# Attention on one core: V loaded in 8 KB runs, reordered by ScalarE and turned by VectorE instead of shuffled by matmuls

## The chip, the cores and the metric

The kernel runs on one core of a Trainium2 chip. Times are device microseconds (us) of a whole execution. An execution can fall in a slower state (for a program on one core: over 1.5% above the fastest run of the same kernel). A profile covers one execution and gives its **span**, which is 1.7 to 3.1 us shorter than the time of the same run. Engines: PE is TensorE, PEld its weight loads, DVE VectorE, ACT ScalarE, POOL GpSimd, SP SyncE; a q after a name is the queue of the engine that issues transfers.

## The reference

```
q, k, v: (32, 12, 128, 64) float32, normal * 0.1
scores = q @ k^T / sqrt(64)
attn   = exp(scores - max);  attn /= sum(attn) + 1e-8
out    = attn @ v            # float32
```

There are 384 heads of 128 rows by 64. Both kernels leave out the maximum (the scores are small) and work in bf16. They read 37.75 MB and write 12.58 MB, 50.3 MB in all. A **step** is 32 heads; there are twelve, 0 to 11, and each loads 1.05 MB each of Q, K and V and stores 1.05 MB.

## The kernel before

Q, K and V are loaded by GpSimd's queue, which casts f32 to bf16 on the way; only the first V comes uncast by two other queues. A Q or K row of 8 KB (a quarter of a head, 32 rows) goes to one partition. V comes in runs of 2 KB (8 rows), and 448 matmuls with a 0/1 matrix `perm` put it in order; ScalarE casts their results back from PSUM (on-chip accumulator memory).

```
def load_v(m):                                   # 2 KB runs, 512 of them
    ...
    nc.gpsimd.dma_start(
        out=chunks[m // 2, 2][:, m % 2 * CB:(m % 2 + 1) * CB],
        in_=vr[:, m * CB:(m + 1) * CB, :].rearrange("p n (t d) -> p n t d", t=T))
...
def turn(m, which):                              # VectorE: 32x32 blocks of 4-byte words
    ...
    nc.vector.transpose(
        xt.rearrange("p h (x g) -> p x h g", g=4),
        x if which == 0 else x.rearrange("p (y t) e -> p t y e", t=T))
...
def values(m, a, heads, half):                   # V's shuffle
    ...
                nc.tensor.matmul(
                    v_ps[u * 32:(u + 1) * 32, i], lhsT=perm[:, a + i, tl, :],
                    rhs=v_bf[:, ns, 2 * u + tl, :], start=(tl == 0), stop=(tl == 1), ...)
    nc.scalar.copy(v2s[m][:, a:a + heads, ns], v_ps)
```

The main loop is software-pipelined: step m+1's scores and exponentials (`scores`, two halves) stand beside step m's denominators and outputs. Each half has one matmul group, then one exponential of 128x2048. The order in the program is the order on each engine. Stores of finished steps are held back by about five steps (LAG), and loads are issued five steps ahead (AHEAD):

```
held = {m: [m - LAG] for m in range(LAG, e - 3)}             # e = 11
between = {(e - 3, 0): [e - 8], (e - 3, 1): [e - 7], (e - 2, 0): [e - 6],
           (e - 2, 1): [e - 5, e - 4], (e - 1, 0): [e - 3]}
...
for m in range(NDUO):
    if m < e:
        scores(m + 1, 0)
    for s in between.get((m, 0), []):
        store(s, nc.scalar)
    divide(m, denominators(m))
    ...
    finish(m, 0, outputs(m, 0))
    ...
    if m < e:
        scores(m + 1, 1)
    ...
    finish(m, 1, outputs(m, 1))
    ...                                          # turn(m + 2), load(later[m]), scale, held stores
```

The softmax here doesn't subtract the row's maximum and nothing guards it: scores larger than these inputs give would overflow.

## Time and profile before

| | before |
|---|---|
| time, median of the first three runs | 128.65 us (127.93 to 129.0) |
| span of the profiled run | 126.1 us |
| mean granted clock of TensorE | 0.863 |
| first exponential of step 1 / of step 11 | 18.78 / 110.02 us |
| last load landed | 107.3 us |

The page's busy row and the row of the clock that TensorE was granted, before. In the first, each engine has its busy time, its share of the span and its instructions; in the second the span is cut into 40 slices, and each digit is tenths of the full clock.

```profile
PE 71.4 (57%) x2080; PEld 42.4 (34%) x2080; DVE 78.2 (62%) x79; ACT 69.8 (55%) x50; POOL 64.2 (51%) x54
PEclk9999999975699995999965799859999558999855
```

No compute engine is busy for more than 62% of the span, and the clock is mostly full. The DMA row, its GB/s and the chain are shown in the prediction below. The GB/s count bytes as they are written: a cast load of 210 GB/s reads 420, a store of 420 writes 420.

### The profile page before, as it was taken

What the parts mean: (1) busy time and instruction counts of PE and PEld (TensorE: products, weight loads), DVE (VectorE), ACT (ScalarE), POOL (GpSimd) and SP (SyncE); (2) the same over time, 40 slices, a digit from 0 to 9 for tenths busy, and PEclk for the clock granted to TensorE, in tenths of its full rate; (3) what the DMA queues carried; (4) which work ended last, traced back from release to release, by engine and by line L of the source; (5) the groups of instructions that cost most, each with busy time, mean ns of one, the idle gap of its engine ahead of it and who ended that gap; (6) DMA issues with size and microseconds to landing.
All of it is one profiled execution on the core that took longest, in us unless ns stands there. A gap on an engine that the chain in (4) does not pass through costs nothing.

```text
span 126.1 us, 4462 instructions
## 1 busy us (share of the span) xinstructions
PE 71.4 (57%) x2080; PEld 42.4 (34%) x2080; DVE 78.2 (62%) x79; ACT 69.8 (55%) x50; POOL 64.2 (51%) x54
## 2 busy tenths in 40 slices
PE   0001977658975738866279857486653588654200
PEld 0001655423533424534046244334240345342100
DVE  1333438745385968559962959584686387496950
ACT  4110896915497734877556777339576148773000
POOL 6941123215942999169881782900916500929510
PEclk9999999975699995999965799859999558999855
DMA  3999999999999999999999999999999999999974
GB/s 98 318 213 217 200 217 209 201 197 219 200 214 211 218 210 204 208 223 205 215 200 222 209 225 316 273 352 211 218 275 316 314 344 385 418 429 426 377 329 199
DMA packets 11699, 32.27 MB, mean 256 GB/s; under 512 B 800, under 2 KB 6432, under 8 KB 10272
## 3 DMA queue, kind: packets, MB, share of 16 engines
q0 software_dynamic: 9264, 18.35, 77.5%
q10 hardware_dynamic: 1712, 10.49, 20.5%
q1 hardware_dynamic: 704, 3.15, 6.4%
q8 instruction: 16, 0.26, 0.7%
q14 instruction: 3, 0.02, 0.0%
HBM read 37.75 MB, written 12.58 MB: 399 GB/s over the span
## 4 chain that ended last, share of the span: by engine, by line
DMA 80%; DVE 5%; issue 4%; ACT 3%; POOL 2%; PE 2%; DVEq 0%; ACTq 0%; POOLq 0%
DMA k_bf<-in_k_dram 42%; DMA v_bf<-in_v_dram 32%; DMA q_bf<-in_q_dram 5%; ACT attn L121 3%; DVE o_sb L176 2%; DVE o_sb L181 1%; POOL o_sb L181 1%; PE s_ps L116 1%; DVE dt L169 1%; DVE kt L104 1%; POOL v_bf L65 1%; PE d_ps L147 1%; DVEq L271 0%; POOL k_bf L57 0%; DVE recip L171 0%
## 5 line engine op out<-in xcount | busy, mean ns | idle before, releaser
L121 ACT ACTIVATE attn<-s_ps 128x2048 bf16<-128x2048 f32 x24 | 45.1, 1879 | 26.8 <-PE s_ps L116 26.7
L181 POOL TENSOR_TENSOR o_sb<-o_sb,recip 128x2048 f32<-128x2048 f32 (+1 forms) x13 | 41.9, 3229 | 25.5 <-DVE o_sb L176 21.7
L116 PE MATMUL s_ps<-qt,kt 32*128 32x128 bf16 x768 | 17.8, 235 | 37.3 <-DVE kt L104 30.9
L176 DVE STREAM_TRANSPOSE o_sb<-o_ps 128x1024 f32<-128x1024 f32 x24 | 28.7, 1214 | 11.3 <-PE o_ps L157 11.3
L136 PE MATMUL v_ps<-v_bf,perm 128*32 128x512 bf16 (+1 forms) x448 | 31.8, 421 | 6.1 <-DVE dt L169 3.1
L140 ACT CAST v<-v_ps 128x1024 bf16<-128x1024 f32 x24 | 24.0, 1014 | 13.6 <-PE v_ps L136 13.5
L116 PEld LDWEIGHTS <-kt 32*128 32x128 bf16 x768 | 13.6, 101 | 47.3 <-DVE kt L104 35.7
L169 DVE STREAM_TRANSPOSE dt<-d_ps 128x1024 f32<-128x1024 f32 x12 | 15.0, 1250 | 18.9 <-PE d_ps L147 18.9
L136 PEld LDWEIGHTS <-perm 128*32 128x32 bf16 x448 | 13.9, 110 | 18.1 <-issue 13.1
L157 PE MATMUL o_ps<-attn,v 128*32 128x128 bf16 x768 | 17.9, 241 | 1.4 <-DVE dt L169 0.9
L104 DVE STREAM_TRANSPOSE kt<-k_bf 128x1024 f32<-128x1024 f32 x12 | 14.6, 1217 | 4.4 <-DMA k_bf<-in_k_dram 4.4
L104 DVE STREAM_TRANSPOSE qt<-q_bf 128x1024 f32<-128x1024 f32 x12 | 14.5, 1209 | 3.3 <-DMA q_bf<-in_q_dram 3.3
L157 PEld LDWEIGHTS <-v 128*32 128x32 bf16 x768 | 14.3, 107 | 6.1 <-issue 3.3
L57 POOL DMA_DIRECT2D k_bf<-in_k_dram x12 | 6.8, 563 | 12.7 <-DMA v_bf<-in_v_dram 8.1
L57 POOL DMA_DIRECT2D q_bf<-in_q_dram x12 | 6.9, 572 | 12.0 <-DMA v_bf<-in_v_dram 7.3
L65 POOL DMA_DIRECT2D v_bf<-in_v_dram x11 | 8.5, 770 | 5.7 <-DMA v_bf<-in_v_dram 2.4
L147 PE MATMUL d_ps<-attn,ones 128*32 128x512 bf16 x96 | 9.1, 435 | 1.2 <-ACT attn L121 0.9
L171 DVE RECIPROCAL recip<-dt 128x32 f32<-128x32 f32 x12 | 4.2, 354 | 0.8
L94 ACT CAST v_bf<-raw 128x1024 bf16<-128x1024 f32 x1 | 1.0, 1045 | 3.2 <-DMA raw<-in_v_dram 3.2
L147 PEld LDWEIGHTS <-ones 128*32 128x32 bf16 x96 | 1.7, 96 | 3.3 <-issue 2.4
L181 DVE TENSOR_TENSOR o_sb<-o_sb,recip 128x512 f32<-128x512 f32 x2 | 2.0, 1053 | 0.0
L94 ACT ACT_TABLE_LOAD x1 | 1.3, 1283 | 1.3 <-PEq L260 1.3
(10 smaller groups left out, 2.3 us busy)
## 6 DMA issues: line engine op xcount, KB each, us to landing
out_dram<-o_sb ACTq DMA_DIRECT2D x9, 1024.0 KB, 10.0
q_bf<-in_q_dram POOLq DMA_DIRECT2D x12, 512.0 KB, 20.0
k_bf<-in_k_dram POOLq DMA_DIRECT2D x12, 512.0 KB, 20.0
v_bf<-in_v_dram POOLq DMA_DIRECT2D x11, 512.0 KB, 20.9
out_dram<-o_sb SPq DMA_DIRECT2D x2, 1024.0 KB, 7.3
raw<-in_v_dram ACTq DMA_DIRECT2D x1, 512.0 KB, 5.0
raw<-in_v_dram SPq DMA_DIRECT2D x1, 512.0 KB, 4.6
out_dram<-o_sb ACTq DMA_DIRECT2D x1, 512.0 KB, 2.9
```

The lines of the kernel that those rows point to most:

```text
L57: nc.gpsimd.dma_start(out=x, in_=(qr, kr)[which][:, m, :].rearrange("p (t d) -> p t d", d=D))
L65: nc.gpsimd.dma_start(out=chunks[m // 2, 2][:, m % 2 * CB:(m % 2 + 1) * CB], in_=vr[:, m * CB:(m + 1) * CB, :].rearrange("p n (t d) -> p n ...
L104: nc.vector.transpose(xt.rearrange("p h (x g) -> p x h g", g=4), x if which == 0 else x.rearrange("p (y t) e -> p t y e", t=T))
L116: nc.tensor.matmul(s_ps[:, b, h, :], lhsT=kt[pr, 4 * i + h, :, j], rhs=qt[pr, 4 * i + h, :, j], start=(j == 0), stop=(j == 1), tile_positi ...
L121: nc.scalar.activation(out=attn, in_=s_ps, func=mybir.ActivationFunctionType.Exp, bias=0.0, scale=scale)
L136: nc.tensor.matmul(v_ps[u * 32:(u + 1) * 32, i], lhsT=perm[:, a + i, tl, :], rhs=v_bf[:, ns, 2 * u + tl, :], start=(tl == 0), stop=(tl == ...
L140: nc.scalar.copy(v2s[m][:, a:a + heads, ns], v_ps)
L147: nc.tensor.matmul(d_ps[b * 32:(b + 1) * 32, 4 * i:4 * i + 4], lhsT=ones, rhs=attns[m, i][:, b], start=True, stop=True, tile_position=(0, ...
L157: nc.tensor.matmul(o_ps[b * 32:(b + 1) * 32, h], lhsT=v2s[m // 2][:, h, 4 * (m % 2) + b, j * 32:(j + 1) * 32], rhs=attns[m, h // 4][:, b, ...
L169: nc.vector.transpose(dt, turned(d_ps))
L176: nc.vector.transpose(o_sb[:, :, j * 32:(j + 1) * 32], turned(o_ps))
L181: eng.tensor_mul(x, x, recip[:, lo:hi].to_broadcast([128, hi - lo, x.shape[2]]))
```

## The change

The intent: V in 8 KB runs like Q and K, so that DMA has fewer and larger packets, and no shuffle on TensorE. A V head's quarter must then go to its own quarter of the partitions, so a V load is four transfers of 32 partitions. ScalarE reorders pairs of bf16 (`order_v`), VectorE turns V (`turn_v`), and K too is now turned plainly and reordered by ScalarE (`order_k`).

```diff
-    def load_v(m):
-        ...
+    vr = v.rearrange("b h (g t) d -> (b h) g (t d)", t=TQ).rearrange("(n p) g x -> p n g x", p=32)
+    def load_v(m, x, engines):
+        for g in range(GQ):
+            engines[g % len(engines)].dma_start(
+                out=x[g * 32:(g + 1) * 32], in_=vr[:, m, g, :].rearrange("p (t d) -> p t d", d=D))
+        return x
...
+        raw = load_v(0, po.tile([128, TQ, D], f32, tag="o_sb", name="raw"), [nc.sync, nc.scalar])
+        load("k0 q0 k1 q1 v1")
...
+        def turn_k(m):
+            xt = pt.tile([128, TQ, 32], f32, tag="kx", name="kx")
+            nc.vector.transpose(xt, chunks.pop((m, 1)).bitcast(f32))
+            qts[m, 2] = xt.bitcast(bf16).rearrange("p x (c j) -> p c x j", j=2)
+        def order_k(m):
+            kt = pt.tile([128, 32, TQ, 2], bf16, tag="kt", name="kt")
+            nc.scalar.copy(kt, qts.pop((m, 2)))
+            ...
+        def order_v(m):
+            vp = pt.tile([128, D // 2, TQ, 2], bf16, tag="vp", name="vp")
+            nc.scalar.copy(vp, chunks.pop((m, 2)).rearrange("p t (r j) -> p r t j", j=2))
+        def turn_v(m):
+            vt = pa.tile([128, D // 2, 32], f32, tag="vt", bufs=2, name="vt")
+            nc.vector.transpose(vt, v2s[m].rearrange("p r t j -> p r (t j)").bitcast(f32))
+            ...
-        def values(m, a, heads, half):
-            ...
         def outputs(m, j):
...
-                        lhsT=v2s[m // 2][:, h, 4 * (m % 2) + b, j * 32:(j + 1) * 32],
+                        lhsT=v2s[m][:, 8 * b + h, :, j],
...
         for m in range(NDUO):
...
             if m < e:
                 scores(m + 1, 1)
...
+            if m + 2 <= e:
+                order_k(m + 2)
+                order_v(m + 2)
+                turn_q(m + 2)
...
+            if m < e:
+                turn_v(m + 1)
+            if m + AHEAD < NDUO:
+                load(f"k{m + AHEAD} q{m + AHEAD} v{m + AHEAD}")
```

The order of stores (`held`, `between`) is unchanged, but that of the loads is not: before, V came two steps at a time, ahead of Q and K, and the last load was step 11's K; now each step loads K, Q and V in this order, and the last load is step 11's V.

More of the change, by code (lines that the diff above doesn't have):

```diff
@@ L5 @@
 from concourse import bass_utils, mybir
-from concourse.masks import make_identity
 from concourse._compat import with_exitstack
@@ L31 @@
     TQ = 32
-    T = 8
-    A = 8
-    CB = 4
+    GQ = S // TQ
     NDUO = B * H // 32
@@ L37 @@
     LAG = 5
-    def runs(x, t):
-        return x.rearrange("b h (g t) d -> (b h g) (t d)", t=t).rearrange(
-            "(n p) x -> p n x", p=128)
-    qr, kr, vr, orr = runs(q, TQ), runs(k, TQ), runs(v, T), runs(out, TQ)
+    qr, kr, orr = (x.rearrange("b h (g t) d -> (b h g) (t d)", t=TQ).rearrange(
+        "(n p) x -> p n x", p=128) for x in (q, k, out))
+    vr = v.rearrange("b h (g t) d -> (b h) g (t d)", t=TQ).rearrange("(n p) g x -> p n g x", p=32)
     singles = ctx.enter_context(tc.tile_pool(name="singles", bufs=1))
@@ L59, in load_qk @@
         chunks[m, which] = x
-    def load_v(m):
-        if m % 2 == 0:
-            chunks[m // 2, 2] = pin.tile([128, 2 * CB, T, D], bf16, tag="v_bf", bufs=3, name="v_bf")
-        nc.gpsimd.dma_start(
-            out=chunks[m // 2, 2][:, m % 2 * CB:(m % 2 + 1) * CB],
-            in_=vr[:, m * CB:(m + 1) * CB, :].rearrange("p n (t d) -> p n t d", t=T))
+    def load_v(m, x, engines):
[3 more added lines that the diff above has]
+        return x
     with tc.manual_schedule():
-        raw = po.tile([128, CB, T, D], f32, tag="o_sb", name="raw")
-        for eng, lo in ((nc.sync, 0), (nc.scalar, CB // 2)):
-            eng.dma_start(out=raw[:, lo:lo + CB // 2], in_=vr[:, lo:lo + CB // 2, :].rearrange(
-                "p n (t d) -> p n t d", t=T))
+        raw = load_v(0, po.tile([128, TQ, D], f32, tag="o_sb", name="raw"), [nc.sync, nc.scalar])
         def load(names):
@@ L77, in load @@
                 kind, m = name[0], int(name[1:])
-                load_v(m) if kind == "v" else load_qk(m, "qk".index(kind))
-        load("q0 k0")
-        ident = singles.tile([128, 128], bf16)
-        make_identity(nc, ident)
-        chunks[0, 2] = pin.tile([128, 2 * CB, T, D], bf16, tag="v_bf", bufs=3, name="v_bf")
-        load("q1 k1 v1")
-        perm = singles.tile([128, A, 2, 32], bf16)
-        nc.vector.memset(perm, 0.0)
-        for tl in range(2):
-            nc.vector.tensor_copy(
-                perm[:, :, tl, tl * 16:(tl + 1) * 16].rearrange("p a (x g) -> p a x g", x=4),
-                ident.rearrange("p (a g x) -> p a x g", a=A, x=4))
+                if kind == "v":
+                    chunks[m, 2] = load_v(
+                        m, pin.tile([128, TQ, D], bf16, tag="v_bf", name="v_bf"), [nc.gpsimd])
+                else:
+                    load_qk(m, "qk".index(kind))
@@ L91 @@
+        load("k0 q0 k1 q1 v1")
         ones = singles.tile([128, 32], bf16)
         nc.vector.memset(ones, 1.0)
-        for lo, cast in ((0, nc.vector.tensor_copy), (CB // 2, nc.scalar.copy)):
-            cast(chunks[0, 2][:, lo:lo + CB // 2], raw[:, lo:lo + CB // 2])
-        load("q2 k2 v2 v3 q3 k3 v4 v5 q4 k4")
-        later = ["q5 k5", "v6 v7 q6 k6", "q7 k7", "v8 v9 q8 k8", "q9 k9", "v10 v11 q10 k10",
-                 "q11 k11"]
-        def turn(m, which):
-            x = chunks.pop((m, which)).bitcast(f32)
-            xt = pt.tile([128, 8, S], f32, tag="qk"[which] + "t", name="qk"[which] + "t")
-            nc.vector.transpose(
-                xt.rearrange("p h (x g) -> p x h g", g=4),
-                x if which == 0 else x.rearrange("p (y t) e -> p t y e", t=T))
-            qts[m, which] = xt.bitcast(bf16).rearrange("p h (s j) -> p h s j", j=2)
+        chunks[0, 2] = raw
@@ new lines, with turn_q @@
+        load("k2 q2 v2 k3 q3 v3 k4 q4 v4")
+        def turn_q(m):
+            xt = pt.tile([128, 8, S], f32, tag="qt", name="qt")
+            nc.vector.transpose(
+                xt.rearrange("p h (x g) -> p x h g", g=GQ), chunks.pop((m, 0)).bitcast(f32))
+            qts[m, 0] = xt.bitcast(bf16).rearrange("p h (s j) -> p h s j", j=2)
+        def turn_k(m):
+            xt = pt.tile([128, TQ, 32], f32, tag="kx", name="kx")
+            nc.vector.transpose(xt, chunks.pop((m, 1)).bitcast(f32))
+            qts[m, 2] = xt.bitcast(bf16).rearrange("p x (c j) -> p c x j", j=2)
@@ new lines, in order_k @@
+        def order_k(m):
+            kt = pt.tile([128, 32, TQ, 2], bf16, tag="kt", name="kt")
+            nc.scalar.copy(kt, qts.pop((m, 2)))
+            qts[m, 1] = kt.rearrange("p (h g) x j -> p h (g x) j", g=GQ)
+        def order_v(m):
+            vp = pt.tile([128, D // 2, TQ, 2], bf16, tag="vp", name="vp")
+            nc.scalar.copy(vp, chunks.pop((m, 2)).rearrange("p t (r j) -> p r t j", j=2))
+            v2s[m] = vp
+        def turn_v(m):
+            vt = pa.tile([128, D // 2, 32], f32, tag="vt", bufs=2, name="vt")
+            nc.vector.transpose(
+                vt, v2s[m].rearrange("p r t j -> p r (t j)").bitcast(f32))
+            v2s[m] = vt.bitcast(bf16).rearrange("p r (h j) -> p h r j", j=2)
@@ L123, in scores @@
             attns[m, i] = attn
-        def values(m, a, heads, half):
-            v_bf = chunks[m, 2]
-            ns = slice(0, 2 * CB) if half is None else slice(half * CB, (half + 1) * CB)
-            if m not in v2s:
-                v2s[m] = pa.tile([128, A, 2 * CB, D], bf16, tag="v2", bufs=2, name="v2")
-            v_ps = ps.tile([128, heads, 4 * CB // heads, D], f32, tag="w_ps", bufs=2, name="v_ps")
-            for i in range(heads):
-                for tl in range(2):
-                    for u in range(4):
-                        nc.tensor.matmul(
-                            v_ps[u * 32:(u + 1) * 32, i], lhsT=perm[:, a + i, tl, :],
-                            rhs=v_bf[:, ns, 2 * u + tl, :], start=(tl == 0), stop=(tl == 1),
-                            tile_position=(0, u * 32))
-            nc.scalar.copy(v2s[m][:, a:a + heads, ns], v_ps)
         def denominators(m):
@@ L164, in turned @@
         def turned(src):
-            return src.rearrange("p h (x g) -> p x h g", g=4)
+            return src.rearrange("p h (x g) -> p x h g", g=GQ)
         def divide(m, d_ps):
@@ L172, in divide, with elements @@
             osbs[m] = (po.tile([128, TQ, D], f32, tag="o_sb", name="o_sb"), recip)
+        def elements(m, j):
+            return osbs[m][0].rearrange("p t (r j) -> p t r j", j=2)[:, :, :, j]
         def finish(m, j, o_ps):
-            o_sb, _ = osbs[m]
-            nc.vector.transpose(o_sb[:, :, j * 32:(j + 1) * 32], turned(o_ps))
+            nc.vector.transpose(elements(m, j), turned(o_ps))
         def scale_rows(m, eng, lo, hi, j=None):
             o_sb, recip = osbs[m]
-            x = o_sb[:, lo:hi] if j is None else o_sb[:, lo:hi, j * 32:(j + 1) * 32]
+            x = o_sb[:, lo:hi] if j is None else elements(m, j)[:, lo:hi]
             eng.tensor_mul(x, x, recip[:, lo:hi].to_broadcast([128, hi - lo, x.shape[2]]))
@@ L191 @@
                    (e - 2, 1): [e - 5, e - 4], (e - 1, 0): [e - 3]}
-        shuffles = {0: [(0, 0, 4, 1), (0, 4, 4, 1)],
-                    1: [(1, a, 2, None) for a in range(0, A, 2)]}
-        for m in range(2, NDUO // 2):
-            shuffles[2 * m - 2] = [(m, 0, 2, None)]
-            shuffles[2 * m - 1] = [(m, a, 2, None) for a in range(2, A, 2)]
-        turn(0, 0)
-        turn(0, 1)
+        turn_k(0)
+        turn_q(0)
+        order_k(0)
         scores(0, 0)
-        values(0, 0, 4, 0)
+        order_v(0)
         scores(0, 1)
-        values(0, 4, 4, 0)
-        turn(1, 0)
-        turn(1, 1)
+        turn_k(1)
+        order_k(1)
+        turn_q(1)
+        turn_v(0)
+        order_v(1)
         for m in range(NDUO):
-            todo = shuffles.get(m, [])
             if m < e:
@@ L211 @@
             divide(m, denominators(m))
-            if len(todo) > 3:
-                values(*todo.pop(0))
+            if m + 2 <= e:
+                turn_k(m + 2)
             finish(m, 0, outputs(m, 0))
-            if len(todo) > 1:
-                values(*todo.pop(0))
             if m < e:
@@ L220 @@
                 store(s, nc.scalar)
-            if m == e - 2:
-                turn(e, 0)
+            if m + 2 <= e:
+                order_k(m + 2)
+                order_v(m + 2)
+                turn_q(m + 2)
             if m >= e - 1:
@@ L225 @@
             finish(m, 1, outputs(m, 1))
-            for x in todo:
-                values(*x)
-            if m + 2 <= e:
-                if m < e - 2:
-                    turn(m + 2, 0)
-                turn(m + 2, 1)
-            if m < len(later):
-                load(later[m])
+            if m < e:
+                turn_v(m + 1)
+            if m + AHEAD < NDUO:
+                load(f"k{m + AHEAD} q{m + AHEAD} v{m + AHEAD}")
             if m < e - 1:
```

## The prediction

> **What bounds the kernel now.** I read the page first, then the DMA rows, then the chain, then each engine's timeline. From the page, slices, queues and shares of the chain:
>
> ```profile
> DMA  3999999999999999999999999999999999999974
> GB/s 98 318 213 217 200 217 209 201 197 219 200 214 211 218 210 204 208 223 205 215 200 222 209 225 316 273 352 211 218 275 316 314 344 385 418 429 426 377 329 199
> q0 software_dynamic: 9264, 18.35, 77.5%
> DMA 80%; DVE 5%; issue 4%; ACT 3%; POOL 2%; PE 2%; DVEq 0%; ACTq 0%; POOLq 0%
> ```
>
> The 16 DMA engines are full from the second slice to the last three, and 80% of the chain is DMA. The loads cast f32 to bf16, so some 210 GB/s written means 420 GB/s read. The trace's packet records give the mean time of a packet by size: 3072 packets of Q and K (8 KB read, 4096 B written) took 324 ns each, 5632 of V (2 KB read, 1024 B written) 98.8 ns. Four V packets carry one Q packet's bytes and take 395 ns: V costs 22% more DMA time per byte. One pair of batches ("step": k, q, v of 32 heads) costs (256 x 324 + 512 x 98.8) / 16 = 8.35 us of each engine.
>
> But the chain of waits names transfers that were early. In the order of time, its last pieces:
>
> ```profile
> 54.67 20.47 DMA k_bf<-in_k_dram
> 75.14 0.29 issue
> 75.43 32.52 DMA k_bf<-in_k_dram
> 107.94 0.02 issue
> 107.97 1.26 DVE kt L104
> ```
>
> Only the last load is truly waited for: it is issued at 75.43 and lands 32.5 us later, because stores began at 72 and share the engines. Before that, VectorE waits for K and Q only 7.7 us in all (groups below, last column), and most of it at the start. So in the middle compute has its own pace. The groups of ScalarE and VectorE:
>
> ```profile
> L121 ACT ACTIVATE attn<-s_ps 128x2048 bf16<-128x2048 f32 x24 | 45.1, 1879 | 26.8 <-PE s_ps L116 26.7
> L140 ACT CAST v<-v_ps 128x1024 bf16<-128x1024 f32 x24 | 24.0, 1014 | 13.6 <-PE v_ps L136 13.5
> L104 DVE STREAM_TRANSPOSE kt<-k_bf 128x1024 f32<-128x1024 f32 x12 | 14.6, 1217 | 4.4 <-DMA k_bf<-in_k_dram 4.4
> L104 DVE STREAM_TRANSPOSE qt<-q_bf 128x1024 f32<-128x1024 f32 x12 | 14.5, 1209 | 3.3 <-DMA q_bf<-in_q_dram 3.3
> L171 DVE RECIPROCAL recip<-dt 128x32 f32<-128x32 f32 x12 | 4.2, 354 | 0.8
> ```
>
> The pace is read from ScalarE's timeline, at the first exponential of each step: 39.47, 46.96, 56.22, 63.71, 73.71, 81.20, 91.18, 100.44, 110.02. That is 8.4 to 8.7 us a step in the middle, 9.3 and 9.6 for the last two. One step, all engines' timeline:
>
> ```profile
> 39.47 1.88 ACT L121 ACTIVATE attn<-s_ps 128x2048 bf16<-128x2048 f32 x1 [0.83 <-PE s_ps L116]
> ...
> 41.40 0.64 PE L116 MATMUL s_ps<-qt,kt 32*128 32x128 bf16 x32 [1.04 <-ACT attn L121]
> ...
> 42.15 1.88 ACT L121 ACTIVATE attn<-s_ps 128x2048 bf16<-128x2048 f32 x1 [0.80 <-PE s_ps L116]
> ```
>
> The scores have one PSUM buffer, so between a step's two exponentials ScalarE has a hole of 0.80 us. From 110.02 to the span's end at 126.1 is a tail of 16.1 us, in which the last step is divided, turned, scaled and stored.
>
> **What the Trainium skill says.** "ScalarE: Activation LUTs", What ACT_TABLE_LOAD costs: an ACTIVATE with immediate operands takes 186 ns + 0.833 ns per element, neighbours overlap by about 93 ns. That gives 1892 and 1039 ns for 2048 and 1024 elements; the trace has 1879 and 1014, and starts 0.93 us apart in a pair of casts (1.94 us for two). It agrees. "SBUF — State Buffer", Door 1: 32 partitions reach 8 of the 16 DMA ports, a ceiling of about 218 GB/s; and lines of 16 bytes want at least two accesses each. No run here shows either yet. The V loads become such quarters; with the cast they write about 210 GB/s at the present rate, just under it. "TensorE: Matmul & The Clock Gate", Part 1: an idle window of about 3.4 us halves the clock. The trace agrees: 32 score matmuls take 0.64 us warm and 1.04 cold, and the clock falls after the pauses.
>
> **The change, part by part.**
>
> DMA. V comes in runs of 8 KB, so 11 loads of 128 packets at 324 ns replace 512 at 98.8: per step 128 x 324 / 16 = 2.59 us for 3.16, in all -6.3 us. The first V, uncast, goes from 512 packets of 2 KB at 100 ns to 128 at about 309: -0.7 us. 33 more transfers end in 16 small packets of 22 ns each: +0.7 us. Sum -6.2 us; a step's load is 7.8 us of packet time, and some 7.5 on the clock, as packets overlap by 5% (before: 132.7 us of packets in 126).
>
> TensorE loses all 448 shuffles (31.8 us busy), which delayed PSUM buffers. No gain by itself: PE isn't the bound.
>
> ScalarE loses 24 casts at 1.014 and one of 1.045, gains 12 K and 12 V copies of 2048 elements. I take 1.88 us each, as a bf16 pair is read from one line each time: +45.1 - 25.4 = +19.7, in all 90 us.
>
> VectorE gains 12 transposes of V at 1.2 (+14.6), loses a cast and the mask (-1.3): 91.5 us. Per step 1.25 + 0.35 + 5 x 1.21 = 7.65, or about 7.3 at overlapping starts.
>
> GpSimd issues four V transfers for one. A 512-row issue took 0.757 us, a 128-row one 0.54: 0.57 ns a row, so 32 rows make about 0.49. Per step 3.63 (scaling) + 2 x 0.54 + 4 x 0.49 = 6.7 us: it fits. Eight load semaphores rotate in both kernels, so eight outstanding transfers now hold 3.5 to 5 MB of input for 8, some 8 us of work at least: more than one scaling.
>
> What binds then is ScalarE's order in a step: exponential, hole, exponential, K copy, V copy. Starts: 1.88 + 0.80 + 1.80 + 1.80 + 1.80 = 8.08 us with a warm TensorE, 0.40 more when cold. PE is busy only 3.1 us of a step with a pause of about 3, so I take it cold half the time: **8.3 us a step**. VectorE's transpose of K must end before the K copy, 4.5 us into the step; its start leaves about 2 us of room, so it doesn't bind.
>
> Start: K's first load lands near 8.1 where Q's did, Q near 10.6. Turn K to 9.4, copy to 11.3, turn Q to 11.9, scores 13.0. Exponentials at 13.05 and, after the first V copy, 16.75; K copy 18.6, V copy 20.4; the step-1 exponential begins at 22.3 (before: 18.78). So 3.5 us are lost here. Ten steps on: 22.3 + 83 = 105.3 for the last step's first exponential, where it was 110.02. With the tail, 16.1 + 0.3 for a colder TensorE, the span is 121.7; the profiled run was 1.9 us above its span and the median 2.5: **124.0 us**.
>
> DMA alone would allow the same: (132.7 - 6.2) x 0.95 = 120, with 1.5 us of start. The last K must land before 98 and the last V before 103: at 7.5 us a step they would land by 92, with the stores issued till then (some 4 x 2.3, partly shared) about 97. It is just in time.
>
> **The rivals.** (1) DMA stays the bound and ScalarE hides: for it the full DMA row, against it the 8.3 us step against 7.5. It would make 121 to 122. (2) ScalarE's or VectorE's strided access costs more: the copies read pairs of bf16 128 bytes apart, the output transposes write every second word. No row of before has this shape. Each 0.2 us on both copies is 0.4 x 10.5 = 4.2 us; copies of 2.3 us would make 132. (3) V's quarters use half the ports and packets stretch: at 400 ns the gain of DMA is gone, and with the late stores the end comes at 126 to 128. (4) PE's weights for the outputs are now strided by 128 bytes: if 0.63 becomes 1.7 us, the room in a step still holds it, but the tail grows by about 1.5.
>
> **Range and chances.** The centre is 124.0. A step off by 0.4 us moves 4 us; hence 120.0 to 129.5, more room upward as rivals 2 to 4 all add. Faster by over 2% means under 126.1: 0.65. Within 2%: 0.27. Slower: 0.08.
>
> **What would show it.** Right: V packets of 4096 B at 324 to 340 ns; K and V copies of 1.85 to 1.95 us; first exponentials 8.1 to 8.5 us apart, with ScalarE's idle mostly the 0.8 us holes; the second step's at 22; ScalarE about 90 us busy, VectorE 92; the DMA row with gaps after 90 us. Wrong: copies above 2.1 us, output transposes above 1.4, ScalarE waiting for K's transpose or for V's landing, or the last V landing after 103.

## The result, and the profile after

The changed kernel took **134.87 us** (median of four runs, 134.11 to 135.71) against 128.82 us (127.93 to 129.55). The ratio is **1.047** (95% interval 1.038 to 1.057): it is slower. Ratios here are the mean time of one kernel's fast runs over that of the other's of the same rounds, so not quite the ratio of the medians quoted. The profiled span went from 126.1 to 132.7 us, the mean clock from 0.863 to 0.691.

From the page after: busy row, clock, DMA rows in 40 slices of 3.3 us, the row of the casting queue, and the chain's shares.

```profile
PE 57.4 (43%) x1632; PEld 41.1 (31%) x1632; DVE 89.3 (67%) x87; ACT 90.5 (68%) x49; POOL 77.1 (58%) x85
PEclk9999999999955558655577555555556856955555
DMA  4999999999999999999999999999999999991752
GB/s 109 223 211 214 214 207 216 210 212 211 211 212 214 212 209 214 212 211 211 211 215 190 276 281 279 296 218 322 310 309 317 322 331 393 400 415 54 311 214 112
q0 software_dynamic: 5568, 18.35, 69.7%
DMA 64%; POOL 13%; DVE 10%; issue 5%; PE 2%; ACT 1%; DVEq 0%; ACTq 0%; POOLq 0%
```

The casting queue's share fell from 77.5% to 69.7%, as intended. Yet the middle of the GB/s row is the 210 that it was. The DMA row stays full until slice 36, where before it was full till slice 38 of a shorter span. Then it breaks: 54 GB/s in slice 37, with 311, 214 and 112 behind it. TensorE runs at half clock for most of the span.

The groups of ScalarE and VectorE after (line, engine, operation, names and shapes, count, then busy us and mean ns, then the idle time before them with its releaser):

```profile
L122 ACT ACTIVATE attn<-s_ps 128x2048 bf16<-128x2048 f32 x24 | 45.1, 1881 | 13.5 <-PE s_ps L117 13.5
L162 DVE STREAM_TRANSPOSE o_sb<-o_ps 128x1024 f32<-128x1024 f32 x24 | 28.9, 1206 | 5.6 <-PE o_ps L141 5.6
L95 ACT COPY kt<-kx 128x2048 bf16<-128x2048 bf16 x12 | 23.5, 1961 | 8.1 <-DVE kx L90 8.1
L100 ACT COPY vp<-v_bf 128x2048 bf16<-128x2048 bf16 x11 | 22.2, 2017 | 6.4 <-DMA v_bf<-in_v_dram 6.4
L90 DVE STREAM_TRANSPOSE kx<-k_bf 128x1024 f32<-128x1024 f32 x12 | 14.4, 1196 | 10.2 <-DMA k_bf<-in_k_dram 10.2
```

The busy times came out close to the prediction. The last-but-one row has something new: ScalarE waits 6.4 us for a landing of V. ScalarE's timeline shows which one (start, duration, instruction, and in brackets the idle time before it and its releaser):

```profile
100.53 1.88 ACT L122 ACTIVATE attn<-s_ps 128x2048 bf16<-128x2048 f32 x1
103.21 1.88 ACT L122 ACTIVATE attn<-s_ps 128x2048 bf16<-128x2048 f32 x1 [0.80 <-PE s_ps L117]
104.98 1.93 ACT L95 COPY kt<-kx 128x2048 bf16<-128x2048 bf16 x1
113.29 1.99 ACT L100 COPY vp<-v_bf 128x2048 bf16<-128x2048 bf16 x1 [6.37 <-DMA v_bf<-in_v_dram]
...
115.17 1.88 ACT L122 ACTIVATE attn<-s_ps 128x2048 bf16<-128x2048 f32 x1
118.25 1.88 ACT L122 ACTIVATE attn<-s_ps 128x2048 bf16<-128x2048 f32 x1 [1.20 <-PE s_ps L117]
```

The copy of step 11's V (`order_v(m + 2)`) waited 6.37 us for the last load, and both exponentials of step 11, which do not need V, stood behind it on ScalarE. Now they start at 115.17; before, the first of them came at 110.02, when the last V had been in since 90.2 us (packet records):

```profile
110.02 1.88 ACT L121 ACTIVATE attn<-s_ps 128x2048 bf16<-128x2048 f32 x1 [0.57 <-PE s_ps L116]
```

The hole between the two is now 1.20 us, the one of a cold TensorE (half clock), for 0.80 with a warm one. What this does to DMA is seen in two windows of each kernel (from and to, length, then busy us and count of PE, PEld, DVE, ACT and POOL, the clock, the DMA share, where 1 is all 16 engines, and GB/s). Before:

```profile
117.00:120.00 3.00, 0.50 (x32) 0.33 (x24) 2.96 (x4) 0.00 (x0) 1.71 (x2) 0.81 0.91 374
120.00:123.00 3.00, 0.00 (x0) 0.00 (x0) 1.57 (x2) 0.00 (x0) 0.42 (x1) 0.50 0.78 322
```

After:

```profile
117.00:120.00 3.00, 2.48 (x68) 1.78 (x68) 0.80 (x1) 1.80 (x2) 0.00 (x0) 0.50 0.88 369
120.00:123.00 3.00, 1.93 (x48) 1.26 (x51) 2.90 (x4) 0.13 (x1) 1.93 (x1) 0.50 0.07 27
```

Before, DMA is still at work on stores while the last step is computed. After, it runs dry from 120 to 123 us: everything that could be stored had been, and the last outputs were not ready.

A count of the packet records gives the same picture in megabytes, loads (by bytes read) and stores together. At 9 us 2.6 MB had moved before and 2.0 after; at 75 us 30.0 and 29.5; at 111 us 45.0 and 44.5; at 117 us 47.5 and 46.9; at 123 us 49.6 and 48.2. The two kernels move bytes at nearly the same pace up to 117 us; the changed one starts 0.6 MB behind and loses the rest at the end.

### The profile page after: what moved, and what is told of

The parts are those of the page before. It is cut to its first block, busy times and chain, and to the rows that moved or that the text cites. A ratio compares the mean times of both kernels' runs of the same rounds, so it can differ in the third digit from the quotient of the medians.

```text
span 132.7 us, 3647 instructions
## 1 busy us (share of the span) xinstructions
PE 57.4 (43%) x1632; PEld 41.1 (31%) x1632; DVE 89.3 (67%) x87; ACT 90.5 (68%) x49; POOL 77.1 (58%) x85
## 3 DMA queue, kind: packets, MB, share of 16 engines
q0 software_dynamic: 5568, 18.35, 69.7%
## 4 chain that ended last, share of the span: by engine, by line
DMA 64%; POOL 13%; DVE 10%; issue 5%; PE 2%; ACT 1%; DVEq 0%; ACTq 0%; POOLq 0%
DMA q_bf<-in_q_dram 47%; DMA v_bf<-in_v_dram 17%; POOL o_sb L167 7%; DVE o_sb L162 4%; POOL v_bf L58 3%; POOL k_bf L52 2%; DVE dt L153 2%; DVE vt L106 2%; ACT attn L122 1%; DVE o_sb L167 1%; DVE qt L84 1%; PE s_ps L117 1%; PE o_ps L141 1%; DVEq L250 0%; POOL q_bf L52 0%
## 5 line engine op out<-in xcount | busy, mean ns | idle before, releaser
L122 ACT ACTIVATE attn<-s_ps 128x2048 bf16<-128x2048 f32 x24 | 45.1, 1881 | 13.5 <-PE s_ps L117 13.5
L117 PE MATMUL s_ps<-qt,kt 32*128 32x128 bf16 x768 | 23.6, 286 | 64.0 <-ACT kt L95 20.9
L117 PEld LDWEIGHTS <-kt 32*128 32x128 bf16 x768 | 18.6, 125 | 68.5 <-ACT kt L95 45.4
L58 POOL DMA_DIRECT2D v_bf<-in_v_dram x44 | 21.9, 500 | 29.3 <-DMA q_bf<-in_q_dram 15.5
L95 ACT COPY kt<-kx 128x2048 bf16<-128x2048 bf16 x12 | 23.5, 1961 | 8.1 <-DVE kx L90 8.1
L100 ACT COPY vp<-v_bf 128x2048 bf16<-128x2048 bf16 x11 | 22.2, 2017 | 6.4 <-DMA v_bf<-in_v_dram 6.4
L141 PE MATMUL o_ps<-attn,vt 128*32 128x128 bf16 x768 | 25.0, 300 | 1.8 <-DVE vt L106 0.8
L141 PEld LDWEIGHTS <-vt 128*32 128x32 bf16 x768 | 20.7, 156 | 10.7 <-issue 7.0
L90 DVE STREAM_TRANSPOSE kx<-k_bf 128x1024 f32<-128x1024 f32 x12 | 14.4, 1196 | 10.2 <-DMA k_bf<-in_k_dram 10.2
L106 DVE STREAM_TRANSPOSE vt<-vp 128x1024 f32<-128x1024 f32 x12 | 14.5, 1206 | 0.0
L131 PE MATMUL d_ps<-attn,ones 128*32 128x512 bf16 x96 | 12.8, 621 | 0.6 <-ACT attn L122 0.6
```

What stands on the lines that cost most here:

```text
L58: engines[g % len(engines)].dma_start(out=x[g * 32:(g + 1) * 32], in_=vr[:, m, g, :].rearrange("p (t d) -> p t d", d=D))
L95: nc.scalar.copy(kt, qts.pop((m, 2)))
L100: nc.scalar.copy(vp, chunks.pop((m, 2)).rearrange("p t (r j) -> p r t j", j=2))
L106: nc.vector.transpose(vt, v2s[m].rearrange("p r t j -> p r (t j)").bitcast(f32))
L117: nc.tensor.matmul(s_ps[:, b, h, :], lhsT=kt[pr, 4 * i + h, :, j], rhs=qt[pr, 4 * i + h, :, j], start=(j == 0), stop=(j == 1), tile_positi ...
L122: nc.scalar.activation(out=attn, in_=s_ps, func=mybir.ActivationFunctionType.Exp, bias=0.0, scale=scale)
```

## The experiments

All were run in three rounds beside the kernel before on the same chip. Spans are of the profiled run. "Wrong" marks kernels that compute a wrong result on purpose. Medians are of all runs, ratios of fast ones alone; of the four runs two were slow in b_no_stores and one each in a_v11_late and a_kdirect.

| run | what | span | median | ratio to before (95%) |
|---|---|---|---|---|
| l_v2k (wrong) | loads only, V in 2 KB runs | 97.4 | 99.19 | 0.769 (0.766 to 0.773) |
| l_v8k (wrong) | loads only, V in 8 KB runs | 97.2 | 98.94 | 0.768 (0.764 to 0.771) |
| b_v_quarters | before, each V load in four | 128.5 | 129.37 | 1.002 (0.996 to 1.008) |
| a_raw_halves | after, first V's quarters dealt otherwise | 132.6 | 134.89 | 1.048 (1.043 to 1.053) |
| a_v0_cast | after, first V through the casting queue | 133.7 | 135.51 | 1.053 (1.049 to 1.057) |
| a_no_stores (wrong) | after, five stores dropped | 127.9 | 129.13 | 1.002 (0.998 to 1.006) |
| b_no_stores (wrong) | before, five stores dropped | 123.1 | 125.48 | 0.966 (0.959 to 0.973) |
| a_no_stores_warm (wrong) | as a_no_stores, unused matmuls | 125.2 | 127.50 | 0.993 (0.985 to 1.001) |
| a_no_stores_kdirect (wrong) | as a_no_stores, no K copy | 117.3 | 119.42 | 0.928 (0.925 to 0.931) |
| a_v11_late | after, last V copy behind the exponentials | 131.0 (slow) | 132.58 | 1.027 (1.020 to 1.033) |
| a_stores_late | after, stores two to three steps later | 130.9 | 132.67 | 1.031 (1.026 to 1.035) |
| b_sched | before, stores later | 130.7 | 132.10 | 1.029 (1.025 to 1.032) |
| a_kdirect | after, no K copy | 134.6 (slow) | 135.71 | 1.054 (1.049 to 1.060) |
| a_sched | after, last V copy late, stores later | 133.2 | 134.97 | 1.048 (1.040 to 1.055) |
| a_kdirect_sched | a_sched and no K copy | 127.3 | 128.81 | 1.004 (0.999 to 1.008) |
| a_kdirect_sched_v0 | and first V through the casting queue | 126.3 | 128.16 | 0.999 (0.996 to 1.002) |

My **theory** after reading the traces: DMA gained nothing from the larger runs, both kernels sit on the same bytes, and the changed one loses because its chain of compute is longer and its last V lands late. The **rivals**: the quarters of V (32 partitions each, eight transfers outstanding) make DMA slower; the slow first V sets the loss; ScalarE's longer work alone sets it; or the cold clock does.

### Do larger runs save DMA time?

Two kernels only load: twelve times Q, K and V with the cast, freed by tiny copies, and one small store.

```diff
+        for m in range(NDUO):
+            if m >= 4:
+                use(m - 4)          # three copies of one element per partition
+            load_qk(m, 0)
+            load_qk(m, 1)
+            load_v(m)               # l_v8k: four transfers of 8 KB runs
```

> Wrong on purpose: nothing but the loads of the kernel before (all 37.7 MB with the cast, V in 2 KB runs), each chunk touched once by VectorE, one row stored. To be set against its twin with V in 8 KB runs. If a packet's duration is what it costs the engine, as the prediction took it: 12 x 8.35 = 100 us of loading. If the bytes set the time, at the 414 GB/s read that the kernel before showed between 12 and 69 us: 91 us. Some 5 us of start and end come on top.

> Wrong on purpose: the twin with the changed kernel's loads, V in 8 KB runs and four transfers. By packet durations 12 x 7.8 = 93.6 us, 6 us less than its twin; by bytes at the 419 GB/s that the changed kernel showed, 90 us, 1 to 2 us less. If four transfers for one or the eight semaphores starve the engines, it is not faster at all.

From the pages of the two, l_v2k first:

```profile
span 97.4 us, 171 instructions
q0 software_dynamic: 9792, 18.88, 104.1%
```

```profile
span 97.2 us, 224 instructions
q0 software_dynamic: 5760, 18.88, 98.1%
```

The packet time (share times span) fell from 101.4 to 95.4 us, and the span by 0.2 us. A share of 104% tells why: an engine's records overlap, since a packet's record begins before its neighbour's has ended. The mean duration of a packet (98.8 ns for the small ones, 326 for the large) is thus no price. The windows from 12 to 69 us of the two full kernels say the same; before, then after:

```profile
12.00:69.00 57.00, 40.17 (x1164) 24.29 (x1168) 36.30 (x35) 37.82 (x28) 31.65 (x27) 0.87 1.13 209
```

```profile
12.00:69.00 57.00, 29.23 (x864) 21.44 (x865) 43.65 (x43) 49.47 (x28) 35.96 (x46) 0.76 1.06 212
```

A DMA share of 1.13 for 209 GB/s became 1.06 for 212. By the packet records the reads were at 414 and 419 GB/s. The Trainium skill, "HBM Reference", Specifications, says that a core which streams alone reaches about 425 GB/s, bounded by its 16 DMA engines; both kernels agree, and with that the change had nearly nothing to win here. The skill's "DMA: Bandwidth & Descriptors", Why small descriptors are slow, names a fixed overhead of about three cycles a packet beside one cycle per 32 bytes. On the written side that is 35/32 against 131/128 for V, 7% of a third of the bytes, some 2 us of 97 as an estimate; the runs show 0.2.

The other side of the same question puts quarters into the kernel before:

```diff
-        nc.gpsimd.dma_start(
-            out=chunks[m // 2, 2][:, m % 2 * CB:(m % 2 + 1) * CB], ...)
+        for lo in range(0, 128, 32):
+            nc.gpsimd.dma_start(
+                out=chunks[m // 2, 2][lo:lo + 32, m % 2 * CB:(m % 2 + 1) * CB], ...)
```

> The kernel before, correct, with each V load cut into four transfers of 32 partitions (same 2 KB runs), as the change does. If four transfers for one cost something by themselves (eight outstanding transfers hold half the bytes, GpSimd issues 33 more): over 1 us slower, or a dip in the DMA row. If not: same within 1 us.

1.002 of before, with an interval that ends at 1.008: four 32-partition transfers for one, and more of them outstanding, cost at most some 1 us. That rival falls as the cause of the 4.7%, though not as a small part of it. The profiled run was the slowest of the five (130.3 us), and by its packet records it fell behind the kernel before between 70 and 95 us, from 0.2 MB to some 0.85 MB.

### The start

```diff
# a_raw_halves
-            engines[g % len(engines)].dma_start(
+            engines[g * len(engines) // GQ].dma_start(
```

> The changed kernel with one edit: the first V's quarters are dealt so that the two queues write different halves of the partitions (quarters 0 and 1 on one queue, 2 and 3 on the other), instead of both starting in the lower half. If the 576 ns of its 8 KB packets come from two queues writing the same ports: packets fall to 310 to 350 ns, the first V is in by about 5.3 us for 7.0, the first K's turn begins near 8.4 us for 9.8, and the whole gets 1 to 1.5 us shorter (about 133.4). Rival, a start limit of the engines or of HBM with 8 KB packets: packets stay above 500 ns and nothing moves.

The first V's packets (8 KB, uncast) took 576 ns each in the changed kernel and 513 here, where 309 had been predicted; V had landed at 6.64 us instead of 7.04 (5.32 before the change). The whole time did not move (1.048).

Why the packets are slow is only inferred: the Trainium skill, "SBUF — State Buffer", "Can I just issue two DMAs to hit both halves?", says that two concurrent transfers at partitions 0 and 64 measured only 6% over a single one. Here dealing the quarters to the other halves gave 11% on the packets; it agrees in kind. From the first packet to the last, the first V took 5.3 us in the changed kernel, 4.9 here and 3.5 before the change. (The 228 GB/s in the next expectation come from packet durations, 128 x 576 / 16 = 4.6 us; over the 5.3 us it is 199.)

The next run takes the slow packets away instead.

```diff
# a_v0_cast
-        raw = load_v(0, po.tile([128, TQ, D], f32, tag="o_sb", name="raw"), [nc.sync, nc.scalar])
...
-        load("k0 q0 k1 q1 v1")
+        load("k0 q0 v0 k1 q1 v1")
-        chunks[0, 2] = raw
```

> The changed kernel, but the first V too is loaded with the cast by GpSimd, behind the first K and Q, not uncast by two queues ahead of them. If the slow start (8 KB packets of 576 ns, 228 GB/s for that MB) is the f32 write of 32 partitions at a time: no packet is slow any more, the first K's turn begins near 7 us for 9.8, the step-1 exponential near 21 us for 23.7, the span falls 1 to 2.5 us unless the last V's landing hides it. Rival, the start is slow whatever is loaded: first K at 9 or later.

It has no slow packets. VectorE's first turn of K began at 6.43 us instead of 9.80, and the first exponential of step 1 at 20.84 instead of 23.73. Still the kernel was not faster (1.053): ScalarE's copy of the last V waited 7.39 us and began at 113.92, and step 11's exponentials came at 115.82. **Compute that starts 2.9 us earlier only waits longer at the end**: what sets the end here is when the last V lands (its last packet ended at 113.29 us; 112.5 in the changed kernel), behind the same bytes.

### Compute alone

Dropping the stores of steps 0 to 4 takes 5.2 MB from the queue ahead of the last loads. What remains shows the compute chain nearly alone.

```diff
         def store(m, eng, lo=0, hi=TQ):
+            if m < 5:
+                return
```

> Wrong on purpose: the changed kernel without the stores of steps 0 to 4, 5.2 MB or some 12 us of DMA work less. Theory 1, stores that share the engines make the last V late and that is the extra time: the last V lands near 101, ScalarE's idle before the last V copy (6.4 us) goes, first exponentials stay 8.5 us apart to the end, span about 126.5 (time about 128.5). Theory 2, DMA bounds throughout: the span falls by the whole 11 to 12 us, to 121. Theory 3, neither: under 3 us.

> Wrong on purpose: the kernel before without the stores of steps 0 to 4, to see its own pace of compute. If the last two steps (9.3 and 9.6 us) waited for loads that share the engines with stores: they fall to 8.7, the last first exponential is near 107, span about 123.5. If they are compute: no change beyond 1 us.

The last exponentials' first halves, from ScalarE's timelines of a_no_stores and then b_no_stores:

```profile
110.30 1.88 ACT L122 ACTIVATE attn<-s_ps 128x2048 bf16<-128x2048 f32 x1
```

```profile
106.98 1.88 ACT L121 ACTIVATE attn<-s_ps 128x2048 bf16<-128x2048 f32 x1
```

In a_no_stores no V copy waits any more, so the 6.37 us did come from the stores ahead of the last load. But the changed kernel is then still 4.8 us longer than the old one under the same treatment (127.9 against 123.1). The parts: step 1's exponential at 23.85 against 18.60, so +5.25 at the start; ten steps of 8.65 against 8.84, so -1.9; a tail of 17.6 against 16.1, so +1.5. **The change made the pace a little better and the start and tail worse.**

Is the cold clock a part? In a_no_stores_warm, 24 unused matmuls per step write to a buffer that the denominators overwrite.

```diff
+        def warm(m, n):
+            dps[m + 1] = ps.tile([128, 8, S], f32, tag="w_ps", bufs=2, name="d_ps")
+            for i in range(n):
+                b = i % 4
+                nc.tensor.matmul(dps[m + 1][b * 32:(b + 1) * 32, 0:4], lhsT=ones,
+                                 rhs=attns[m + 1, 0][:, b], start=True, stop=True, ...)
...
             finish(m, 1, outputs(m, 1))
+            if m < e:
+                warm(m, 24)
```

> Wrong on purpose, like the changed kernel without the stores of steps 0 to 4 (127.9 us of span), plus 24 unused matmuls on TensorE after each step's outputs, only to keep its clock up. If the cold clock lengthens the holes between exponentials (1.2 us for 0.8): clock share near 0.95 for 0.67, nearly all holes 0.80, first exponentials 8.3 us apart for 8.65, span 2.5 to 4 us shorter (124 to 125.5). Rival, the clock is beside the path or the extra work delays the scores: under 1 us.

The clock went from 0.673 to 0.912, the holes between exponentials to 0.80 us, the step from 8.57 to 8.33 us (both over the nine steps from 1 to 10), and the span from 127.9 to 125.2. By the ratios to before (0.993 over 1.002) the gain is about 0.9%. So the cold clock is a term of 1 to 3 us of compute, not the cause. In the whole kernels it hardly shows: the changed kernel's run at a mean clock of 0.871 took 134.11 us and those at 0.69 took 134.51 to 135.71, and the four runs of a_sched had clocks of 0.647, 0.777, 0.881 and 0.913 and took 134.07, 134.97, 135.52 and 134.97 us.

And the K copy? VectorE can write K straight in its order, as words 128 bytes apart:

```diff
         def turn_k(m):
-            xt = pt.tile([128, TQ, 32], f32, tag="kx", name="kx")
-            nc.vector.transpose(xt, chunks.pop((m, 1)).bitcast(f32))
-            ...
+            xt = pt.tile([128, 8, S], f32, tag="kt", name="kt")
+            nc.vector.transpose(
+                xt.rearrange("p h (g x) -> p x h g", g=GQ), chunks.pop((m, 1)).bitcast(f32))
+            qts[m, 1] = xt.bitcast(bf16).rearrange("p h (s j) -> p h s j", j=2)
         def order_k(m):
-            ...
+            pass
```

> Wrong on purpose, without the stores of steps 0 to 4 as above, and with K turned by VectorE straight into its order (writes of one 4-byte word every 128 bytes), so without ScalarE's copy of K. ScalarE's chain gets 1.9 us a step shorter, 6.7 us. If the strided write costs VectorE nothing (1.2 us): steps of 7.7 us or less, VectorE's sum, and a span near 118. If it costs double (2.4 us): VectorE has 8.8 us a step and the span stays at 127 or more.

The group of K's transpose in this run:

```profile
L90 DVE STREAM_TRANSPOSE kt<-k_bf 128x1024 f32<-128x1024 f32 x12 | 23.0, 1916 | 10.2 <-DMA k_bf<-in_k_dram 10.2
```

The scattered write costs 1.916 us against 1.196, so VectorE pays 8.6 us in all; ScalarE loses 23.5 us of copies. The span falls from 127.9 to 117.3 us, and the step to 7.74 us. The K copy was the dearest piece of the changed compute chain that was tried; the copy of V, which is as long, was not taken out.

### Moving the landing and the stores

Three runs change only order.

```diff
# a_v11_late
-                order_v(m + 2)
+                if m + 2 < e:
+                    order_v(m + 2)
...
+            if m == e - 1:
+                order_v(e)
```

> The changed kernel with one edit: ScalarE's copy of the last V stands after the last step's two exponentials instead of before them. If the last V's landing (about 113 us) holds up the exponentials only by ScalarE's order: the last step's first exponential begins near 110 instead of 115, the V copy starts when V lands with no idle before it over 1 us, and the whole is 3 to 4 us shorter (131 to 132). Rival, the last Q and K are as late and the turn of V is what the end waits for: gain under 1 us.

ScalarE's timeline of a_v11_late (only the order and the wait are read):

```profile
111.62 1.88 ACT L122 ACTIVATE attn<-s_ps 128x2048 bf16<-128x2048 f32 x1 [4.07 <-PE s_ps L117]
...
116.57 2.00 ACT L100 COPY vp<-v_bf 128x2048 bf16<-128x2048 bf16 x1
```

The exponentials no longer stand behind V's copy, and the copy finds V landed. They still wait 4.07 us, because step 11's Q is late too: VectorE's turn of it waited for the landing until 109.08 us here, and until 107.30 in the changed kernel. So the late loads still set the start. The time fell to 132.58 us: of the 4.7% lost, 2.1 came back. One misplaced copy is a term of some 2.5 us, and not the whole.

```diff
# a_stores_late (b_sched and the *_sched kernels: likewise, with [3], [4, 5] and [6, 7, 8] in the last three)
-    po = ctx.enter_context(tc.tile_pool(name="po", bufs=LAG + 3))
+    po = ctx.enter_context(tc.tile_pool(name="po", bufs=LAG + 4))
...
-        held = {m: [m - LAG] for m in range(LAG, e - 3)}
-        between = {(e - 3, 0): [e - 8], ...}
+        held = {}
+        between = {(8, 0): [0], (8, 1): [1], (9, 0): [2], (9, 1): [3, 4], (10, 0): [5, 6],
+                   (10, 1): [7, 8]}
```

> The changed kernel, correct, with the stores of the first nine steps issued two to three steps later (and one output buffer more), so that the last loads share the DMA engines with fewer of them. If stores ahead of the last loads are the loss: the last V lands at 98 to 103 for 113, ScalarE has no idle before its last copy, the last step's first exponential begins near 109 to 110 for 115.2, span 127.5 to 129. Rival, the DMA engines' total work bounds: the stores moved to the end make up for it and the span stays above 131.

The last load now lands at 95.7 us, no copy waits for V, and step 11's exponentials start at 110.10. But DMA is short of work from 99 to 105 us (shares of 0.39 and 0.64 in two windows of 3 us), since the loads are done and the first stores come late, and then the stores run until 130 us. It gains 1.6% on the changed kernel and stays 3% above before.

> The kernel before with the same later stores and nothing else, to see how much of any gain is the stores' order. Its own compute alone took 123.1 us of span: if its last two steps waited only for loads behind stores, the span is 123.5 to 125 (2 to 1 us less); if its DMA total bounds, 126 as it was.

The same in the kernel before makes it **worse** (1.029); I had expected a gain or no change. Its DMA row:

```profile
DMA  3999999999999999999999999999997469999991
```

Slices 31 to 33 are not full: the loads ended at 95.5 us and left the engines short of work from 99 to 108. The old order lets stores in while loads are still due, and the kernel before has no such hole in its row.

### The remedies together

> The changed kernel, correct, with K turned by VectorE straight into its order and no copy of K on ScalarE; stores as they were. If ScalarE's pace were what the changed kernel's time hangs on, it would gain as without stores (10 us, to about 124). If the last V's landing sets the end: steps of 7.8 us in the middle, but each step issues its store earlier and the loads fall further behind: the last V still lands near 112, gain 0 to 3 us.

Without the K copy, which was worth 10 us of compute, but with all stores in their old places, the kernel is no faster (1.054). The copy of the last V waits 8.76 us and starts at 115.14. As with a_v0_cast, faster compute waits longer.

> The changed kernel with the two remedies of the landing (later stores, last V's copy behind the last exponentials) but with ScalarE's copy of K kept. With the copy left out as well it was level with before (1.0035). If ScalarE's copy of K counts once the landing no longer binds: first exponentials 8.5 us apart, span 129 to 131, ratio 1.015 to 1.03. If it never counts: 127.3, ratio near 1.00.

With the late last copy and the late stores but the K copy kept, it is no better than the change itself (1.048). Its DMA row, and ScalarE's last copy of V:

```profile
DMA  4999999999999999999999999999996639999991
```

```profile
115.12 1.98 ACT L100 COPY vp<-v_bf 128x2048 bf16<-128x2048 bf16 x1 [1.41 <-POOL o_sb L167]
```

The row has the same hole, from 99 to 111 us, and the last V copy now stands behind three store issues on ScalarE's queue that wait for GpSimd's scaling. I had expected a span of 129 to 131 us; it was 133.2.

> As the one before, and with both remedies of the landing: the first nine stores two to three steps later (spread so that the engines need not run dry, one output buffer more) and the last V's copy behind the last exponentials. If landing and compute are the two limits: the last load lands by 104, the span is 122 to 124.5 (time 124 to 126.5), DMA at 9 tenths to the end. Rival, some third limit: span above 127.

With the K copy gone as well, the late stores leave no hole: the last load lands at 105.5 us, DMA is full to the end, and the time is 128.81 us, level with before (1.004). The expected span of 122 to 124.5 us was missed; it was 127.3.

> As the one before, and the first V loaded with the cast behind K and Q (its start was 2.9 us earlier alone, with no gain in the whole). With the landing no longer the limit that start should now count: 0.5 to 2 us less than the one before; if DMA's total bounds, nothing beyond the 1.4 us of slow first packets.

The DMA row of this last one:

```profile
DMA  1999999999999999999999999999999999999991
```

It is full from the second slice to the last but one, in a span of 126.3 us; the ratio is 0.999 (0.996 to 1.002). Its compute differs much from before's, whose span is 126.1 with nearly as full a row. What they share is 50.3 MB. At the 420 GB/s seen for loads and for stores that is 120 us, with some 3 us until the first bytes and 2 to 3 at the end: an estimate of 125 to 126. No correct kernel of this study had a span under 126.1 us; that none can is not shown. No version was faster than the kernel before, so there is none to recommend.

## Why the prediction was wrong

The direction was wrong: 124.0 us was predicted, faster, and 134.87 came. By the span it is 121.7 predicted against 132.7, 11.0 us more. They add up along the steps of the prediction: the second step's exponential came at 23.73 instead of 22.3 (+1.4); nine steps took 8.53 us each instead of 8.3 (+2.1); the last step took 14.64 us from 100.53 to 115.17 instead of 8.3 (+6.3); the tail took 17.5 instead of 16.4 (+1.1). The sum is 10.9.

**"Sum -6.2 us" for DMA: failed.** The step took the mean duration of a packet as its cost. The packets did become what it said (those of 4096 B, V's among them, took 325.6 ns on average), and the queue's share fell as it said. Loads alone took 97.2 us instead of 97.4. The overlap that the prediction granted, "packets overlap by 5%", was an average over sizes: with V in small packets the share was 1.13 at the full rate, with large ones 1.06, and the rate of 414 to 419 GB/s was the limit in both. The 80% of DMA in the chain and the full DMA row said rightly what bounded the kernel; the gain had to come from fewer bytes, and there were none to save. Rival 1, "DMA stays the bound", was the right thought with the wrong floor: 121 to 122 rather than about 126.

**"-0.7 us for the first V": failed.** The packets were taken at 309 ns and took 576; the first turn of K, whose load is queued behind them, came at 9.80 us instead of the assumed 8.1, and in a_v0_cast, without them, at 6.43. It did not cost the whole its 1.4 us, as a_v0_cast showed, because the end hung on the last landing.

**"The last V before 103 ... It is just in time": failed, and weighed most.** It counted about four stores ahead of the last V and added some 5 us for them. The packet records show 7.4 MB of stores moved by the time that the last load ended, at 112.5 us; seven stores at 2.5 us each are 17 us, not 5. Between 90 and 112.5 us there were 4.1 MB of loads and 5.3 of stores, 9.4 MB in all, at 417 GB/s: nothing was slow, it was simply that much. The prediction did name "the last V landing after 103" as what would make it wrong. It did not look at what stands behind that copy on ScalarE, the last two exponentials. From the landing it was then 20.2 us to the end, with only 5.2 MB (12 us) of stores left to fill them. Before, the last K landed at 107.3, with 6.9 MB (16 us) left for 18.8 us. This is why one DMA row is full at the end and the other broken.

**"In all 90 us" for ScalarE: right in the sum, by some luck, with its terms off.** ScalarE was busy for 90.5 us and VectorE for 89.3 (91.5 predicted). The copies took 1.961 and 2.017 us instead of 1.88, and TensorE was cold in about 60% of the steps instead of half, so holes were 1.20 rather than 0.80. Both are in the 8.53 us a step, just outside the 8.1 to 8.5 foreseen. The start and the tail of the compute are what the sum hid: on equal terms, with five stores dropped, the changed chain is 4.8 us longer than the old.

**Two readings of the kernel before were loose.** Its "8.4 to 8.7 us a step in the middle" is a mean over pairs; by the starts that the prediction lists, single steps alternate between 7.5 and 9.3 to 10.0 us, so the last two, at 9.3 and 9.6, do not stand out singly. And on "the trace agrees" for the clock: that it falls after pauses is right, but in the kernel before it had already fallen to half after four pauses of 2.35 to 2.58 us (and in one of 3.71), shorter than the 3.4 us named.

**Rivals 2 to 4: mostly fell.** The strided output transposes took 1.206 us (1.214 before), as cheap as plain ones. The strided PE weights made weight loads 156 ns against 125 for the scores' in the same kernel, and 32 output matmuls took 1.07 us cold, 1.08 before the change. V's quarters did not stretch with the cast, as the 325.6 ns show; they did without it. GpSimd's issues took 0.500 us (0.49 estimated).

What stays open: a dip between 69 and 80 us. There the packet records have 419 GB/s in the kernel before, but 391 in the changed one (0.3 MB, 0.7 us), 387 in a_v0_cast and 394 in b_v_quarters. V's quarters may have a part in it, though a_kdirect_sched_v0, which has them too, kept 420; the cause was not tested. Nor was the order of the loads: no run keeps the changed kernel but loads V ahead of Q and K, as before. And the cause of the 576 ns packets is argued from a page and not shown.

## What to carry to other kernels

Where the DMA row is full, price a change in bytes over the sustained rate of a window, never in mean packet durations: records overlap, and a change of packet size can move them by 6% and the time by 0.2%. With loads and stores on the same engines, count the bytes that will be ahead of the last load, and see which instructions of an in-order engine stand behind the one that waits for it. And take compute that gets longer at the start and at the end for a loss even where the middle has room, because here DMA ran dry exactly there; test a remedy for the landing and one for the compute together, as each alone may only turn into the other's wait.

## What the Trainium skill lacked or had wrong

- "DMA: Bandwidth & Descriptors" does not say how far the packet records of a trace overlap: casting loads of 2 KB and 8 KB runs had packets of 98.8 and 326 ns, shares of 104.1% and 98.1% of the 16 engines, and spans of 97.4 and 97.2 us. It has no measured comparison of packets of 1 and 4 KB (as written) either; the difference was 0.2 us in 97.
- "HBM Reference" gives 425 GB/s for a core streaming alone, beside 358 for a core whose neighbour streams too. It does not say which side counts when a load casts: 414 to 419 GB/s were sustained for 57 us as bytes read, half of that as bytes written.
- "SBUF — State Buffer", Door 1: no factor for VectorE. It says that an access to each new 16-byte line pays, and the runs agree, but writing one 4-byte word every 128 bytes made a 128x1024 transpose 1.916 us instead of 1.196; writing every second word (1.206) cost nothing.
- "ScalarE: Activation LUTs": its formula gives 1892 ns for 2048 elements, and the exponentials had 1881; copies of bf16 pairs, strided, from one buffer to another took 1961 and 2017, which the section does not cover.
- "SBUF — State Buffer" says that 32 partitions reach half the ports but has no case of four uncast 32-partition transfers from two queues: 128 packets of 8 KB took 576 ns each and 1.05 MB took 5.3 us (199 GB/s), 513 ns and 4.9 us dealt otherwise; with the cast, packets of this size took 325.6 ns.
